# Normalising the input: gamma and beta as columns on transposed blocks, and a first product that goes through feature blocks

## The chip, the cores and the metric

The kernel runs on one core of one Trainium2 chip. The metric is the device time of one execution in microseconds, the median over several runs. A profile is one more execution, recorded instruction by instruction on the same core. The engines are TensorE (PE in the profile, its weight loads PEld), VectorE (DVE), ScalarE (ACT), GpSimd (POOL) and SyncE (SP), whose queue issues all loads here.

## What is computed

The reference is an encoder of two layers on x of 512 tokens by 1024 features. Cut to what matters:

```python
h = layer_norm(x, ln_in_g, ln_in_b)            # (x - mean) * rsqrt(var + 1e-5) * g + b, per token
for l in range(2):
    proj = h @ w_in[l]                         # 1024 x 4608, nine groups of columns
    # differential attention, a gated recurrence in both directions ("hg"), attention into mem
    h = layer_norm(ALPHA * h + mix @ w_out[l], ln1_g[l], ln1_b[l])
    # gated MLP with a depthwise convolution of width 3
    h = layer_norm(ALPHA * h + ffn, ln2_g[l], ln2_b[l])
```

The change concerns the first line and what uses it: `h` is needed twice, as the input of the first projections (features must lie on the partitions, as PE contracts over partitions) and as the residual (tokens on the partitions).

## The kernel before

**Numbers.** Every large product is made of three half-precision ones. A weight of 1 MB is loaded in f32 (`wst`, two buffers), its square is summed on ACT (L262), the sum goes through a tiny product on PE (`stat`, L165) to all partitions, DVE makes a power of two of it (L152 to L156), ACT writes the scaled high part `wh` (L265) and DVE the rest `wl` (L266). The activation has high and low parts `xh` and `xl` likewise, each [128, 8, 512]: feature block k, 512 tokens. A product is `wh·xh + wh·xl + wl·xh` (`mm3`).

**The first norm.** x lies in four tiles `z[0..3]` of 128 tokens by 1024 features. `layernorm(t, 0)` takes one tile: statistics (L222, L224), the reciprocal deviation `rs` in two instructions on POOL (L226, L227), then per half of 512 features two passes with gamma and beta, which lie in full tiles `mix` (a row loaded into all partitions, 512 KB each, L176). For tiles 0 and 1 both passes are on DVE (L235, L236). For tiles 2 and 3 (`LN_POOL`) DVE subtracts and scales (L231), and POOL multiplies by gamma and adds beta (L232, L233). Then PE transposes four blocks of 128 x 128 (L243), ACT writes `xh` with a scale (L247), and DVE `xl` (L248). Tile t is thus finished in `z[t]` for the residual and in `xh`, `xl` at once, and tile 0 can be used while tile 3 has not been touched.

**The first products.** `step_i` (columns 3072 and on of `w_in`, 256 wide) has tokens on the output's partitions: for tile t it runs the eight feature blocks of `wh·xh`, then of `wh·xl`, then of `wl·xh` (the `split` order of `gemm_t`), two tiles to a PSUM bank. `step_qf` takes the two weights after it; in each layer its first call runs the lower 256 tokens of its four outputs and then the upper 256. After it comes `step_fb` (full width, 512), then the keys and values of `mem`, whose blocks are transposed on PE as well (L339), and then the remaining projections. The attention parts are put between projections as a filler.

**What sets the order.** The program is written once in this order. Then a planner (`extract`, `deadlines`, `simulate`) takes all instructions, gives each a cost and a latest time worked back from PE's work, and fills each engine's queue in order of these times among what is ready; for loads it reckons with `DMA_RATE`. The program is built a second time with that order, and with the buffer slots that go with it, fixed for all five queues. So each engine works through its list in order, and a change of the code or of a cost moves instructions everywhere. `START` says what is emitted first: tile 0 of x, gamma and beta, the first weight, tiles 1 and 2, the second weight, tile 3. The order of emission decides between equal times, and who gets a buffer first.

The few lines that matter most, of the norm before:

```python
V.scalar_tensor_tensor(zt[:, c], zt[:, c], mv[:, 0:1], lng[:, c], ALU.subtract, ALU.mult)
V.scalar_tensor_tensor(zt[:, c], zt[:, c], rs, lnb[:, c], ALU.mult, ALU.add)
...
A.activation(xhs, pv, AF.Identity, scale=lnsc[:, idx : idx + 1])
```

## Time and profile before

| | |
|---|---|
| median of 3 runs | 1519.77 us (1518.19 to 1520.24) |
| profiled execution | 1518.81 us |
| its span on the core | 1517.0 us, 24771 instructions |
| mean granted clock of PE | 0.993 |
| loaded from memory | 138.23 MB |

The span is the time from the first to the last instruction of the record; the 1.8 us between it and the execution's time lie around it. A row of a group names the line, the engine, the operation, the tile written, the tiles read, the shapes and the count, then the busy time in us and the mean of one in ns, then the idle time ahead of it and what ended that. A row of the timeline begins with its start and its duration in us. A wait in brackets is the idle time of the engine before the row, and the releaser.

### The profile page before, as it was taken

What the parts mean: (1) busy time and instruction counts of PE and PEld (TensorE: products, weight loads), DVE (VectorE), ACT (ScalarE), POOL (GpSimd) and SP (SyncE); (2) the same over time, 40 slices, a digit from 0 to 9 for tenths busy, and PEclk for the clock granted to TensorE, in tenths of its full rate; (3) what the DMA queues carried; (4) which work ended last, traced back from release to release, by engine and by line L of the source; (5) the groups of instructions that cost most, each with busy time, mean ns of one, the idle gap of its engine ahead of it and who ended that gap; (6) DMA issues with size and microseconds to landing.
All of it is one profiled execution on the core that took longest, in us unless ns stands there. A gap on an engine that the chain in (4) does not pass through costs nothing. (4 is left out here: it accounts for less than half of the span.)

```text
span 1517.0 us, 24771 instructions
## 1 busy us (share of the span) xinstructions
PE 1458.1 (96%) x10072; PEld 823.6 (54%) x10072; DVE 1148.1 (76%) x2133; ACT 860.2 (57%) x1090; POOL 237.2 (16%) x258
## 2 busy tenths in 40 slices
PE   4999999998999999999999999999999999999997
PEld 3776565564574444444478475655555544444443
DVE  7688967868797766776695969678789767666777
ACT  4776555656366555554556556657653656455550
POOL 4131312030011001010110331021201101001011
PEclk9999999999999999999999999999999999999999
DMA  6332121222233333233234212021232333243321
GB/s 223 123 119 84 62 80 56 74 97 71 70 112 111 99 96 111 84 111 101 94 111 140 82 60 85 29 84 56 84 108 72 102 109 108 87 111 104 92 84 56
DMA packets 158141, 141.93 MB, mean 94 GB/s; under 512 B 3286, under 2 KB 139082, under 8 KB 158026
## 3 DMA queue, kind: packets, MB, share of 16 engines
q1 hardware_dynamic: 158026, 140.34, 29.6%
q8 instruction: 79, 1.29, 0.3%
q14 instruction: 36, 0.29, 0.1%
HBM read 138.23 MB, written 2.10 MB: 92 GB/s over the span
## 5 line engine op out<-in xcount | busy, mean ns | idle before, releaser
L137 PEld LDWEIGHTS <-wh 128*128 128x128 f16 x2688 | 256.9, 98 | 233.2 <-issue 3.8
L266 DVE SCALAR_TENSOR_TENSOR wl<-wst,ws,wh 128x2048 f16<-128x2048 f32 x122 | 315.9, 2590 | 72.1 <-ACT wh L265 71.8
L137 PE MATMUL mm<-xh,wl 128*128 128x512 f16 (+1 forms) x832 | 301.7, 363 | 1.3 <-DVE wl L266 1.3
L137 PE MATMUL mm<-xh,wh 128*128 128x512 f16 (+1 forms) x832 | 301.7, 363 | 0.0
L137 PE MATMUL mm<-xl,wh 128*128 128x512 f16 (+1 forms) x832 | 301.6, 363 | 0.0
L262 ACT ACTIVATE wh<-wst 128x2048 bf16<-128x2048 f32 x122 | 232.3, 1904 | 114.5 <-PE stat L165 50.7
L265 ACT ACTIVATE wh<-wst,ws 128x2048 f16<-128x2048 f32 x122 | 243.5, 1996 | 37.2 <-DVE wi L156 20.3
L137 PE MATMUL mm<-wh,t 128*128 128x512 f16 (+1 forms) x768 | 223.1, 370 | 1.7 <-DVE z L529 1.6
L137 PEld LDWEIGHTS <-wl 128*128 128x128 f16 x1344 | 131.6, 98 | 122.2 <-DVE wl L266 1.6
L137 PEld LDWEIGHTS <-t 128*128 128x128 f16 x1152 | 110.4, 98 | 122.1 <-issue 1.2
L529 DVE SCALAR_TENSOR_TENSOR z<-mm,inv,z 128x512 f32<-128x512 f32 x176 | 129.7, 745 | 46.3 <-PE mm L137 32.8
L137 PE MATMUL sc<-xh,wh 128*128 128x512 f16 (+1 forms) x448 | 156.2, 349 | 1.4 <-ACT xh L247 0.8
L137 PE MATMUL sc<-xh,wl 128*128 128x512 f16 (+1 forms) x448 | 156.2, 349 | 0.0
L137 PE MATMUL sc<-xl,wh 128*128 128x512 f16 (+1 forms) x448 | 156.2, 349 | 0.0
L1098 POOL TENSOR_TENSOR t<-f 128x512 f32<-128x512 f32 x44 | 58.1, 1321 | 547.1 <-DVE f L1096 438.5
L137 PE MATMUL mm<-wl,t 128*128 128x512 f16 (+1 forms) x384 | 142.1, 370 | 0.0
L152 DVE TENSOR_SCALAR we<-stat 128x1 int32<-128x1 int32 x122 | 18.4, 151 | 128.0 <-PE stat L165 127.8
L137 PE MATMUL mm<-wh,mgh 128*128 128x512 f16 x192 | 73.4, 382 | 7.8 <-DVE z L529 7.6
L1094 ACT ACTIVATE f<-sc,cvb,cw 128x512 f32<-128x512 f32 x44 | 34.1, 775 | 75.8 <-PE stat L165 72.3
L137 PE MATMUL mm<-wl,mgh 128*128 128x512 f16 x192 | 73.3, 382 | 0.0
L137 PE MATMUL mm<-wh,mgl 128*128 128x512 f16 x192 | 73.1, 382 | 0.0
L986 ACT ACTIVATE f<-sc,dam,iqk 128x512 f32<-128x512 f32 x64 | 49.3, 775 | 37.8 <-DVE dam L984 36.6
(224 smaller groups left out, 2190.5 us busy)
## 6 DMA issues: line engine op xcount, KB each, us to landing
wst<-in_w_up_dram SPq DMA_DIRECT2D x88, 512.0 KB, 4.3
wst<-in_w_in_dram SPq DMA_DIRECT2D x36, 1024.0 KB, 5.2
wst<-in_w_down_dram SPq DMA_DIRECT2D x22, 1024.0 KB, 5.1
wst<-in_w_out_dram SPq DMA_DIRECT2D x12, 1024.0 KB, 5.1
wst<-in_w_mem_kv_dram SPq DMA_DIRECT2D x8, 1024.0 KB, 4.9
z<-in_x_dram SPq DMA_DIRECT2D x4, 512.0 KB
mix<-in_ln_g_dram SPq DMA_DIRECT2D x4, 512.0 KB
mix<-in_ln_b_dram SPq DMA_DIRECT2D x4, 512.0 KB, 3.8
```

The lines of the kernel that those rows point to most:

```text
L137: T.matmul(o, lhsT, rhs, start=start, stop=stop)
L152: V.tensor_scalar(e, tot.bitcast(I32), 0x7F000000, 1, ALU.bitwise_and, ALU.logical_shift_right)
L262: A.activation(h.rearrange("p a b -> p (a b)").bitcast(BF16), flat, AF.Square, accum_out=ss)
L265: A.activation(h.rearrange("p a b -> p (a b)"), flat, AF.Identity, scale=s)
L266: V.scalar_tensor_tensor(l.rearrange("p a b -> p (a b)"), flat, s, h.rearrange("p a b -> p (a b)"), ALU.mult, ALU.subtract)
L529: V.scalar_tensor_tensor(zs, p_, ivs[half % len(ivs)], zs, ALU.mult, ALU.add)
L986: A.activation(pe[:, c, :], sc_[c], AF.Exp, bias=mx[:, c : c + 1], scale=iqk, accum_out=z1 if c else z0)
L1094: A.activation(c, p_, AF.Identity, scale=cw[:, 1, v : v + 1], bias=cvb[:, l, i + 22 * v : i + 22 * v + 1])
L1098: G.tensor_tensor(gt[:, n, :], c2[:, 0, :], c2[:, 1, :], ALU.mult)
```

## The change

- The first norm is a function of its own, `first_norm`. Each tile is only normalised, by one pass on DVE over 1024 features. When all four are done, each feature block k is transposed for all four tiles into one PSUM bank; features are then on the partitions, and ACT applies gamma and beta as columns (scale and bias) and writes f32 `w`; DVE writes `xh` from it and then `xl`.
- The columns `gbc` come from two loads of 4 KB and a transpose (`ln_columns`), and the scale of the first norm is now worked out from them, with a small product on PE.
- The residual gets its gamma and beta apart (`first_affine`): the full tiles are loaded later, and eight passes on DVE over 1024 features (multiply, then add, per tile) run in place on `z`. `proj_scale(0)`, which needs a square of the full gamma, moves with it, to after `step_qf`.
- `step_i` of the first layer has four outputs open, one per tile, in four PSUM banks, and goes through the feature blocks outermost: per block `wh·xh` and `wh·xl` for the four tiles, and after all blocks `wl·xh`.
- `step_qf` runs at full width in the first layer.
- `START`: constants and columns, the four tiles of x, then the two weights. The planner gets a `DMA_RATE` of 370e3 instead of 205e3, and the first nine loads are put ahead of all others.
- `LN_POOL` is gone. The sequence of units (`SEQ`, `LANE`, `LAST`) is now a table with the same content as before. Some small buffers are fewer.

```diff
-START = "0lw12v3"
-LN_POOL = [(0, 2), (0, 3)]
+START = "c0123wv"
...
+    def ln_columns():
+        rows = tmp([P, 160], "crow", bufs=1)
+        for i, v in enumerate(lngb[0]):
+            nc.sync.dma_start(rows[i * KT : (i + 1) * KT, 0:P], v.rearrange("(k p) -> k p", p=P))
+        pt = ptr()
+        T.transpose(pt[:, 0 : 2 * KT], rows[0 : 2 * KT, 0:P], ident[0 : 2 * KT, 0 : 2 * KT])
+        V.tensor_copy(gbc.rearrange("p i k -> p (i k)"), pt[:, 0 : 2 * KT])
...
+        T.matmul(tot, ones, ss.bitcast(BF16)[:, 1:4:2], start=True, stop=True)
+        both = small(2, "gbto", bufs=1)
+        V.tensor_copy(both, tot)
+        ln_scale(both, 0)
+        V.tensor_scalar(gbc, gbc, lnsc[:, 0:1], None, ALU.mult)
+
+    def first_norm():
+        for t in range(TT):
+            mu, rs = norm(t, 0)
+            V.tensor_scalar(z[t], z[t], mu, rs, ALU.subtract, ALU.mult)
+        for k in range(KT):
+            pt = ptr()
+            for t in range(TT):
+                T.transpose(pt[:, t * P : (t + 1) * P], z[t][:, k * P : (k + 1) * P], ident)
+            w = tmp([P, S], "w2", bufs=4)
+            A.activation(w, pt, AF.Identity, scale=gbc[:, 0, k : k + 1], bias=gbc[:, 1, k : k + 1])
+            V.tensor_scalar(xh[:, k, :], w, 1.0, None, ALU.mult)
+            V.tensor_tensor(xl[:, k, :], w, xh[:, k, :], ALU.subtract)
+
+    def first_affine():
+        load_ln(0)
+        for t in range(TT):
+            for j, op in enumerate((ALU.mult, ALU.add)):
+                V.tensor_tensor(z[t], z[t], lngbt[j], op)
...
             def step_qf(ws):
-                if pr == 0:
+                if pr == 0 and l:
...
             def step_i(ws):
-                hs["v"] = yield from tok_out(ws[0], "tokv", l == 0 and pr == 0)
+                if l or pr:
+                    hs["v"] = yield from tok_out(ws[0], "tokv")
+                    return
+                hv = hs["v"] = tmp([P, 4, 256], "tokv", bufs=2)
+                w, iv = ws[0], inv_of(ws[0], xin)
+                ps = [pmm("mm" if t % 2 == 0 else "sc")[:, 0:256] for t in range(TT)]
+                for u, xs in ((w.h, xact), (w.l, xact[:1])):
+                    for k in range(KT):
+                        for n, d in enumerate(xs):
+                            for t in range(TT):
+                                mm(ps[t], d[:, k, t * P : (t + 1) * P], u[:, k, :], u is w.h and k + n == 0, u is w.l and k == KT - 1)
...
-DMA_RATE = 205e3
+DMA_RATE = 370e3
...
+    for k, o in enumerate([o for o in ops if o.dmab][:FIRST]):
+        D[o.i] = k - 1000.0
```

How this moves instructions is seen in each engine's list. SP's list, at the start of the program; `z` are the tiles of x, `wst` weights, `mix` the full gamma and beta, `crow` small rows. Before:

```order
L257 DMA wst_119<-in_w_in_dram 128x8x256
L212 DMA z_77<-in_x_dram 128x1024
L176 DMA mix_100<-in_ln_in_g_dram 128x1024
L176 DMA mix_104<-in_ln_in_b_dram 128x1024
L140 DMA cst<-in_consts_dram 128x132
L212 DMA z_78<-in_x_dram 128x1024
L212 DMA z_79<-in_x_dram 128x1024
L257 DMA wst_136<-in_w_in_dram 128x8x256
L212 DMA z_80<-in_x_dram 128x1024
```

and now:

```order
L143 DMA cst<-in_consts_dram 128x132
L240 DMA crow_99<-in_ln_in_g_dram 8x128
L240 DMA crow_99<-in_ln_in_b_dram 8x128
L218 DMA z_77<-in_x_dram 128x1024
L218 DMA z_78<-in_x_dram 128x1024
L218 DMA z_79<-in_x_dram 128x1024
L218 DMA z_80<-in_x_dram 128x1024
L302 DMA wst_129<-in_w_in_dram 128x8x256
L302 DMA wst_144<-in_w_in_dram 128x8x256
L178 DMA mix_621<-in_ln_in_g_dram 128x1024
```

The four tiles of x moved ahead of both weights, and the full gamma behind them. On DVE, at the second weight's low part (`wl_148` before, `wl_156` now; its product is the first of `step_qf`). Before, `z_80` is the last tile of x and `xl<-tr_225` belongs to the third:

```order
L248 SCALAR_TENSOR_TENSOR xl<-tr_215,lnsc,xh 128x4x128
L463 COPY rpf_1549<-qsc 128x1
L231 TENSOR_SCALAR z_80<-z_80,bnmv_235,lnrs_237 128x512 x2
L266 SCALAR_TENSOR_TENSOR wl_148<-wst_136,ws_144,wh_138 128x2048
L248 SCALAR_TENSOR_TENSOR xl<-tr_225,lnsc,xh 128x4x128
L401 TENSOR_TENSOR w_57_316<-w_56_314 128x256
```

and now, where the rows on `z` are affine passes with gamma, and the last two feature blocks stand some fifteen rows ahead of these:

```order
L443 TENSOR_REDUCE lsum<-w_66_323 128x4
L458 CAST masks<-crow_617 128x160
L272 TENSOR_TENSOR z_77<-z_77,mix_621 128x1024
L155 TENSOR_SCALAR we_344<-stat 128x1
L272 TENSOR_TENSOR z_78<-z_78,mix_621 128x1024
L311 SCALAR_TENSOR_TENSOR wl_156<-wst_144,ws_152,wh_146 128x2048
```

All of `xl` now stands ahead of the second weight's low part, and two affine passes stand between. On PE, at the first transposes. Before, tile 0's two banks are followed by products at once:

```order
L165 MATMUL stat<-wss_122,ones 128x1
L243 MATMUL tr_162<-cst,z_77 128x128 x4
L243 MATMUL tr_171<-cst,z_77 128x128 x4
L137 LDWEIGHTS xh
L137 MATMUL mm_361<-wh_121,xh 128x256
```

and now, where `tr_195` and `tr_204` are feature blocks 0 and 1, each with a piece of all four tiles:

```order
L262 MATMUL tr_195<-cst,z_79 128x128
L262 MATMUL tr_204<-cst,z_79 128x128
L168 LDWEIGHTS ones
L168 MATMUL stat<-wss_132,ones 128x1
L262 MATMUL tr_195<-cst,z_80 128x128
L262 MATMUL tr_204<-cst,z_80 128x128
L262 MATMUL tr_213<-cst,z_77 128x128
```

The sum of the first weight's square (`stat<-wss_132`) moved from the head of PE's list to behind the third tile's transposes, and no product stands ahead of the fourth tile's. The sum of the third weight's square, `stat<-wss_341`, stands among the products of `wl`, after the first five.

More of the change, by code (lines that the diff above doesn't have):

```diff
@@ L169, in trunk @@
     lnsq = [None, None]
-    hold = [None]
     def load_ln(idx):
@@ L247, in layernorm @@
                 A.activation(xhs, pv, AF.Identity, scale=lnsc[:, idx : idx + 1])
-                hold[0] = V.scalar_tensor_tensor(xls, pv, lnsc[:, idx : idx + 1], xhs, ALU.mult, ALU.subtract).ins
+                V.scalar_tensor_tensor(xls, pv, lnsc[:, idx : idx + 1], xhs, ALU.mult, ALU.subtract)
     def prep(src, shape):
@@ L378, in setup_gates @@
             A.activation(e1, e1, AF.Exp)
-            zz = small(4, "lbz")
+            zz = small(4, "lbz", bufs=2)
             V.tensor_tensor(zz, e0, e1, ALU.add)
@@ L458, in scale_rope @@
     def scale_rope(l):
-        f = small(1, "rpf")
+        f = small(1, "rpf", bufs=1)
         if l:
@@ L719, in step_qf @@
                 for i in range(4):
-                    if pr == 0:
+                    if pr == 0 and l:
                         p_ = ps[i]
@@ L1040, in build_layer @@
         if l == 0:
-            add([], lambda ws: [layernorm(t, 0) for t in range(TT)] and None)
-            add([], lambda ws: late(setup_gates))
-            add([], lambda ws: late(proj_scale, 0))
+            add([], lambda ws: first_norm())
+            add([], lambda ws: setup_gates())
         else:
             add_mkv(l)
-        hg_units(0)
-        if l == 0:
-            add([], lambda ws: setup_rope())
-        add([], lambda ws: scale_rope(l))
-        hg_units(1)
-        mx_units(0)
-        mx_units(1)
-        da_units(0)
-        add_wout("hg", 0)
-        da_units(1)
-        add_wout("hg", 1)
-        add_wout("da", 0)
+        for name, *arg in SEQ[l]:
+            if name == "rope":
+                if l == 0:
+                    add([], lambda ws: setup_rope())
+                add([], lambda ws: scale_rope(l))
+            elif name == "out":
+                add_wout(*arg)
+            else:
+                {"hg": hg_units, "mx": mx_units, "da": da_units}[name](*arg)
         ol = {}
@@ L1494 @@
 PEN = 20.0
+FIRST = 9
 def deadlines(ops, tiles):
```

88 lines of the change are left out of this document (51 added, 37 removed).

## The prediction

> **What bounds the kernel now.** I read the page's busy times first, then the same in stretches, then the waits of TensorE (PE).
>
> ```profile
> PE 1458.1 (96%) x10072; PEld 823.6 (54%) x10072; DVE 1148.1 (76%) x2133; ACT 860.2 (57%) x1090; POOL 237.2 (16%) x258
> 0.00:20.00 20.00, 3.29 (x15) 2.48 (x16) 11.32 (x25) 8.63 (x10) 2.93 (x10) 1.00 0.92 327
> 20.00:40.00 20.00, 15.38 (x117) 11.26 (x116) 17.66 (x42) 11.29 (x20) 15.24 (x12) 1.00 0.35 111
> 40.00:60.00 20.00, 20.00 (x186) 17.74 (x185) 11.15 (x45) 14.23 (x18) 0.00 (x0) 1.00 0.35 112
> 60.00:80.00 20.00, 18.35 (x157) 10.84 (x156) 17.43 (x35) 14.38 (x17) 5.26 (x5) 0.93 0.33 107
> 80.00:120.00 40.00, 39.80 (x609) 28.10 (x607) 35.27 (x76) 28.47 (x36) 15.05 (x18) 0.99 0.42 139
> ```
>
> The columns of the stretches are PE, PE's weight loads, VectorE (DVE), ScalarE (ACT), GpSimd (POOL), granted clock, DMA share, GB/s. PE is busy 1458.1 of 1517.0 us, so 58.9 us of idle PE are all that can be won without less work. Of these 21.3 lie in the first 40 us (16.71 + 4.62); from 40 us on PE is full. The change is about these 40 us, so the question is when PE becomes full. The timeline of PE shows its waits there, and where the step after the first two products begins.
>
> ```profile
> 14.78 1.97 PE L243 MATMUL tr<-cst,z 128*128 128x128 f32 x8 [6.65 <-DVE z L236]
> 18.85 1.89 PE L137 MATMUL mm<-wh,xh 128*128 128x256 f16 x8 [2.10 <-ACT xh L247]
> 20.53 2.02 PE L137 MATMUL mm<-wh,xl 128*128 128x256 f16 x8
> 22.34 0.60 PE L137 MATMUL mm<-wl,xh 128*128 128x256 f16 x3
> 34.52 0.28 PE L137 MATMUL mm<-xh,wl 128*128 128x256 f16 x1 [1.33 <-DVE wl L266]
> 37.04 0.66 PE L243 MATMUL tr<-cst,z 128*128 128x128 f32 x4 [0.94 <-POOL z L233]
> 61.13 0.27 PE L137 MATMUL sc<-xl,wh 128*128 128x256 f16 x1
> 61.24 0.27 PE L137 MATMUL sc<-xh,wl 128*128 128x256 f16 x1
> 61.35 0.38 PE L137 MATMUL mm<-xh,wh 128*128 128x512 f16 x1
> 61.57 0.38 PE L137 MATMUL mm<-xl,wh 128*128 128x512 f16 x1
> ```
>
> The last wait ends at 37.04. At 61.35 the first 512-wide product starts: that is `step_fb`, so `step_i` and `step_qf` are done. 61.35 is my mark: whatever is before it, the same step must begin in the changed kernel, and the gain is the difference. Spacing gives a product's price on a full PE: 0.11 us at width 256 (61.13 to 61.24), 0.216 at 512 (61.35 to 61.57 and on).
>
> **The change, part by part.** First the start of the data.
>
> ```profile
> 0.72 0.43 SPq L257 DMA_DIRECT2D wst<-in_w_in_dram  x1
> 10.40 0.25 SPq L363 DMA_DIRECT2D crow<-in_da_norm_g_dram  x1
> 5.91 1.91 ACT L262 ACTIVATE wh<-wst 128x2048 bf16<-128x2048 f32 x1 [3.91 <-DMA wst<-in_w_in_dram]
> 8.24 1.28 DVE L222 BATCH_NORM_STATS2 bnst<-z 128x6 f32<-128x512 f32 x2
> GB/s 7 311 390 307 398 416 362 373 384 322 119 350 100 0 0 4 8 26 359 140 41 0 0 0 136 378 42 303 221 0 0 0 110 377 50 274 250 0 0 8
> ```
>
> (GB/s in slices of 2 us.) Before, the first 1 MB weight is issued at 0.72 and usable 5.19 us later; x's first tile is worked on at 8.24. Now the constants (0.43) and two small loads (0.25 each) go ahead, and x's first tile (0.5 MB) is issued at about 1.9. At about 360 GB/s half a MB less is 1.45 us less: usable at 1.9 + 5.2 − 1.45 = 5.6, the next ones 1.45 apart (10.0 for the fourth). The weights follow at about 12.8 and 15.7 (1 MB is 2.9 us more each). The first one's square ends near 14.9, and the blocks need ACT only at 17, so I cost that at nothing; a weight 2 us later would show in full. The two loads of gamma and beta as full tiles move behind the weights and are hidden.
>
> Now the durations, from the groups by shape, and the spread of three of them.
>
> ```profile
> L222 DVE BATCH_NORM_STATS2 bnst<-z 128x6 f32<-128x512 f32 x40 | 27.0, 685 | 0.2
> L224 DVE BATCH_NORM_AGGREGATE bnmv<-bnst 128x2 f32<-128x12 f32 x20 | 4.1, 205 | 0.1
> L505 DVE TENSOR_SCALAR mgh<-mix,gs 128x1024 f16<-128x1024 f32 x12 | 9.5, 795 | 0.2
> L696 DVE TENSOR_SCALAR f<-sg 128x512 f32<-128x512 f32 x16 | 6.8, 424 | 0.3
> L950 DVE TENSOR_TENSOR sg<-sg,mm 128x512 f32<-128x512 f32 x16 | 10.9, 682 | 5.9 <-POOL sg L948 5.9
> L760 DVE TENSOR_TENSOR t<-f,qg 128x1024 f32<-128x1024 f32 x8 | 15.6, 1956 | 0.0
> L154 DVE TENSOR_SCALAR ws<-we 128x1 int32<-128x1 int32 x122 | 18.3, 150 | 2.9
> L266 DVE SCALAR_TENSOR_TENSOR wl<-wst,ws,wh 128x2048 f16<-128x2048 f32 x122 | 315.9, 2590 | 72.1 <-ACT wh L265 71.8
> L1094 ACT ACTIVATE f<-sc,cvb,cw 128x512 f32<-128x512 f32 x44 | 34.1, 775 | 75.8 <-PE stat L165 72.3 <-PE sc L137 3.5
> L265 ACT ACTIVATE wh<-wst,ws 128x2048 f16<-128x2048 f32 x122 | 243.5, 1996 | 37.2 <-DVE wi L156 20.3 <-DVE ws L154 13.3 <-DVE ge L152 3.3
> L328 ACT ACTIVATE t<-t 128x512 bf16<-128x512 f32 x4 | 2.5, 622 | 0.0
> L226 POOL TENSOR_SCALAR lnrs<-bnmv x20: 221/777/785, 9.9 to 1510.7; 128x1 f32<-128x1 f32 x20
> L227 POOL TENSOR_TENSOR lnrs<-lnrs,mhalf x20: 567/578/2524, 10.7 to 1511.5; 128x1 f32<-128x1 f32 x20
> L231 DVE TENSOR_SCALAR z<-z,bnmv,lnrs x4: 536/542/1492, 22.0 to 30.6; 128x512 f32<-128x512 f32 x4
> L236 DVE SCALAR_TENSOR_TENSOR z<-z,lnrs,mix 128x512 f32<-128x512 f32 x36 | 26.1, 744 | 2.7 <-POOL lnrs L227 2.7
> ```
>
> Step 1, to the fourth normalised tile, on DVE: 8 statistics at 0.64 (two took 1.28) = 5.1; 4 aggregates, 0.8; 4 subtract-and-scale passes 1024 wide, which the trace lacks: between 0.80 (L505, one scalar) and 1.08 (two L231), I take 0.85 = 3.4, near the row of the same width; seven one-column operations of the gamma scale at 0.15 = 1.05; 0.9 for waits on POOL's `rs` (0.22 + 0.57 when free). 5.6 + 11.25 = 16.9.
>
> The pair on POOL is where a rule speaks against the change. L231 took up to 1.49 beside POOL's work and 0.54 free. The Trainium skill, "SBUF — State Buffer", "Who interferes with whom", says that such a DVE pass and GpSimd lock each other out of a shared port for a whole instruction. By it the last `rs` waits for a pass, 0.85 more, and the sum below would be 3.5 instead of 4.4. I keep the row of the free pair, since PE's order needs the last `rs` only once.
>
> Step 2: all four tiles must be there before any block is, unlike before, where tile 0 alone gave products at 18.85. Transposes 0.5, two blocks on ACT at 0.775 (L1094, PSUM with scale and bias columns), the weight's `wh` 2.0: 20.9. Then DVE makes this weight's `wl` ahead of the other six blocks: 2.5 (2.59 mean, 2.35 at best): 23.4.
>
> Step 3: six blocks of 0.42 (L696) + 0.68 (L950), overlapping by 0.06, 1.04 each: 29.7. PE's part (8 products and 4 transposes a block, 1.3) runs beside it.
>
> Step 4: ACT from 20.9: six blocks 4.65, the second weight's square 2.0, four squares of `mem` 2.5, the third weight's square 2.0: 32.1. PE's order puts the sum of that square after five of the 32 `wl` products, so 27 × 0.109 = 2.95 remain, and four transposes of `mem`, 0.45: PE begins `step_qf` at 35.5.
>
> Step 5: DVE from 29.7: eleven one-column operations at 0.15 and three of 256 columns or fewer at 0.4, near L696's row, 2.8 in all; two of the new affine passes, 2.4 (one 1024 wide taken as twice L950 less one overhead, 1.22; L760 shows 1.96 with POOL beside it, and POOL has nothing then), then the second weight's `wl` 2.5: 37.4. PE needs it after four products, at 36.4, and waits 1 us.
>
> Step 6: 92 products of 0.216 remain: 19.9. `step_fb` starts at 57.3 instead of 61.35, 4.0 sooner, and four transposes (0.44) that stood behind it are done. **Gain 4.4 us.**
>
> Cheap ends of the rows (0.80, 2.35, blocks overlapping more) give 5.6; dear ones (1.08, 0.78 for every L226, 2.59, no overlap) 1.9. Neither end falls below zero, because x arrives 2.6 us sooner than before.
>
> The other edits. Work that goes off the path: six more affine passes (7.3 us of DVE) lie in 38 to 56 us, where DVE has 8.85 us free (40 to 60). POOL loses its passes over z, and with them the wait at 37.04:
>
> ```profile
> L232 POOL TENSOR_TENSOR z<-z,mix 128x512 f32<-128x512 f32 x4 | 8.2, 2058 | 2.2 <-DVE z L231 2.2
> L233 POOL TENSOR_TENSOR z<-z,mix 128x512 f32<-128x512 f32 x4 | 5.2, 1312 | 0.0
> ```
>
>  Joining the half-wide products of `step_qf` leaves 0.2. `DMA_RATE` and `FIRST` move weight loads and reorder nearly every engine later on; two buffers hold the weights either way, so I cost that at 0, between −2 and +2: 37.6 us of idle PE (58.9 − 21.3) lie after 40 us, and the largest group there is eight waits for DVE's residual adds:
>
> ```profile
> PE mm L137 <- DVE z L529: 9.1, 8, 2.7
> ```
>
> **The rivals.** First, the gain is given back at the memory products. DVE has 9.2 us more to do (8 affine passes 9.8, 8 for `xh` 3.4, 4 normalising 3.4, the scale 1.0; gone are 8 passes like L236, 5.9, and four L231, 2.5 of them) and was 87% busy from 60 to 80, where PE already waited here:
>
> ```profile
> 76.76 0.71 PE L339 MATMUL tr<-cst,t 128*128 128x128 f32 x4 [1.33 <-issue]
> ```
>
> In its new order DVE has from 37.4 to the last piece of `mem`: five `wl` 12.7, six affine passes 7.3, one L760 1.96, 21 passes of about 0.6 (L696, L950) 12.4, and 54 small operations, 5.9 where they overlap (0.11): 40.3, so 77.7. PE, running free, wants that piece 18.5 after `step_fb` starts (its 48 products 10.4, then 8.1), at 75.8. With the small ones at 0.15 it is ready at 79.9. So PE waits 1.9 to 4.1 instead of 1.3: at the worst 2.8 lost, 1518.2, and with the dear ends of the start 1520.7. Against it: before, DVE's idle time there is mostly waiting for ACT and PE, which now come sooner. Chance 0.23.
>
> Second, slower: the affine passes run at L760's 1.96, 5.9 us more in all. This decides if POOL reads SBUF beside them; POOL's order has nothing between the four `rs` and the gate chain, so that it needs passes slipping past 60 us. Then DVE is the bound up to the gate chain: 15.1 us more work against 8.85 free leaves 6.3 late, 2.8 more at `mem`, less 4.4: 4.7 slower, 1524.5. Chance 0.10.
>
> Third, a clock that stays low. At 18.85 and 20.53 sixteen products took 3.49 us, 0.218 each, twice the 0.109 they take from 22.34 on, though the granted clock reads 1.00. In the new order products come in bursts behind blocks. If they stay at 0.218 until the blocks end, 64 products are 14.0 and 16 transposes 4.0: 39.0 instead of 30.1, less the slack of 2 us before the sum in step 4, 7 late: 1522. The Trainium skill, "TensorE: Matmul & The Clock Gate", "What's actually happening", has PE at half clock until a window of about 3.4 us was busy; the trace's 3.49 agrees. Against the rival: at half speed a block costs PE 2.7 us and DVE 1.04, so PE is busy without a gap and warms up by 24.5, inside the slack. Chance 0.05.
>
> Fourth, later waits shrink with the new order: 2 to 4 us more, 1511 to 1513. Chance 0.10.
>
> **How the numbers follow.** The profiled execution took 1518.81, 0.96 below the median of 1519.77. Span 1517.0 − 4.4 = 1512.6, with 1.8 around it 1514.4; against the median 1519.77 − 4.4 = 1515.4. The forecast has 0.52. Its own bounds are 1513.5 to 1518 (gain 1.9 to 5.6, and the reorder). The range takes in the fourth case's 1511, the first one's 1520.7 and the near half of the slow cases: 1510.5 to 1521.5. About 0.2% (3 us) is what a measurement of this kernel tells from no change. Faster by that means below 1516.7: most of the forecast, all of the fourth: 0.59. Slower means above 1522.8: 0.12. Same: 0.29.
>
> **What would show it.** Right: x's first statistics at 5 to 6; the fourth pass done by 17 to 18; last `xl` near 30; `step_fb` at 56 to 59; DVE busier than 18 of 20 us from 20 to 60. Wrong: first block after 20; PE waiting over 3 us for `wl` near 36 or for `mem` near 75; products 0.218 apart after 27; idle PE after 100 us that differs by more than 3 us.

## The result and the profile after

| | before | after |
|---|---|---|
| median of the runs | 1518.99 us (1518.19 to 1520.24) | 1531.96 us (1528.92 to 1533.23) |
| profiled execution, span | 1518.81, 1517.0 | 1531.11, 1529.3 |
| PE busy, mean granted clock | 1458.1, 0.993 | 1463.1, 0.992 |
| PE idle in the first 100 us | 23.2 | 16.6 |
| PE idle after that | 35.7 | 49.6 |

The changed kernel is slower: ratio 1.0082, 95% interval 1.0064 to 1.0100. (A fourth run brings the median of the kernel before from 1519.77 to 1518.99. One execution of `rate_back` and one of `wl_cost`, both below, ran at a granted clock of 0.943 and 0.698; these two count in the medians and not in the ratios.) The forecast was 4.4 us less; it is 13 us more. The last two rows say where to look. The start won 6.6 us, more than forecast, and everything behind it lost: 13.9 us of waits and 5.0 us of PE's busy time (−6.6 + 13.9 + 5.0 = 12.3, the difference of the spans).

First the start. The busy line and the stretches of the changed kernel, same columns as before (PE, PEld, DVE, ACT, POOL, clock, DMA share, GB/s):

```profile
PE 1463.1 (96%) x9978; PEld 813.2 (53%) x9978; DVE 1141.4 (75%) x2146; ACT 861.7 (56%) x1092; POOL 231.9 (15%) x250
```

```profile
0.00:20.00 20.00, 6.05 (x24) 3.93 (x25) 13.53 (x37) 7.58 (x8) 3.88 (x14) 1.00 0.86 319
20.00:40.00 20.00, 20.00 (x149) 14.96 (x148) 19.90 (x53) 17.87 (x32) 0.00 (x0) 1.00 0.38 126
40.00:60.00 20.00, 20.00 (x97) 9.12 (x96) 18.35 (x51) 14.39 (x16) 0.00 (x0) 1.00 0.49 158
60.00:80.00 20.00, 17.36 (x221) 13.03 (x220) 19.11 (x29) 16.68 (x20) 10.38 (x6) 1.00 0.33 107
80.00:120.00 40.00, 40.00 (x598) 25.05 (x596) 35.68 (x84) 29.18 (x40) 8.17 (x18) 1.00 0.34 113
```

PE is now full from 20 to 60 us, where before it was full only from 40 on; from 60 to 80 it is idle for 2.6 us, a little more than the 1.7 of before. The steps one by one, in the timeline of the changed kernel:

```profile
5.58 1.29 DVE L227 BATCH_NORM_STATS2 bnst<-z 128x6 f32<-128x512 f32 x2 [1.27 <-DMA z<-in_x_dram]
12.54 2.60 DVE L258 TENSOR_SCALAR z<-z,bnmv,lnrs 128x1024 f32<-128x1024 f32 x3
12.97 0.46 POOL L231 TENSOR_SCALAR lnrs<-bnmv 128x1 f32<-128x1 f32 x1
13.52 0.77 POOL L232 TENSOR_TENSOR lnrs<-lnrs,mhalf 128x1 f32<-128x1 f32 x1
25.93 1.29 DVE L266 TENSOR_TENSOR xl<-w,xh 128x512 f16<-128x512 f32 x2
31.52 2.35 DVE L311 SCALAR_TENSOR_TENSOR wl<-wst,ws,wh 128x2048 f16<-128x2048 f32 x1
33.28 0.38 PE L140 MATMUL mm<-xh,wh 128*128 128x512 f16 x1
```

The four normalised tiles are there at 15.1 (12.54 + 2.60), the last `xl` at 27.2, the second weight's `wl` at 33.9, and `step_qf` begins at 33.28. With 96 products of 0.216 it ends at 54.0, and `step_fb` begins at 54.05, where before it began at 61.35.

Now the rest. Three groups of PE's waits after the first 100 us grew (us in all, times, longest):

```profile
PE mm L140 <- DVE z L569: 14.6, 11, 2.7
PE tr L168 <- ACT t L536: 5.5, 4, 1.5
PE stat L168 <- ACT wh L307: 4.0, 7, 1.1
```

Before, the first of them was 9.1 (the eight waits for the residual adds in the prediction), and of the other two there was nothing of note in that stretch. That is 15 us more, about the 13.9 of all waits together. The last two come from ACT. These are the waits of ACT ahead of a weight's square, by what ended them, of the kernel before and of the changed one (us, times):

```profile
  DMA wst<-in_w_up_dram: 11.0, 4
  DMA wst<-in_w_in_dram: 6.5, 3
  DMA wst<-in_w_mem_kv_dram: 2.1, 1
```

```profile
  DMA wst<-in_w_up_dram: 36.4, 18
  DMA wst<-in_w_down_dram: 18.8, 8
  DMA wst<-in_w_in_dram: 16.5, 7
  DMA wst<-in_w_out_dram: 2.4, 2
  DMA wst<-in_w_mem_kv_dram: 0.5, 2
```

19.6 us of waits for weights have become 74.5 (10.1 of them stand at the very start, where x goes first). The loads are no slower: where the trace shows a landing, it came 3.6, 4.8 and 6.2 us after the issue (the least, the median and the most of 40 loads, half of them of 512 KB), against 3.9, 5.0 and 11.7 before (23 loads). The squares stand where the loads have not landed yet. What that does is seen in the second MLP, in SP's queue of loads of the kernel before, then of the changed one:

```profile
1306.26 10.41 SPq L257 DMA_DIRECT2D wst<-in_w_down_dram  x2
1368.60 10.41 SPq L257 DMA_DIRECT2D wst<-in_w_down_dram  x2
1430.94 31.15 SPq L257 DMA_DIRECT2D wst<-in_w_down_dram  x4
```

```profile
1310.85 10.41 SPq L302 DMA_DIRECT2D wst<-in_w_down_dram  x2
1376.52 9.76 SPq L302 DMA_DIRECT2D wst<-in_w_down_dram  x2
1441.52 30.50 SPq L302 DMA_DIRECT2D wst<-in_w_down_dram  x4
```

One round of six weights took 62.34 us before, both times, and takes 65.7 and 65.0 now. PE was busy for the whole of those 62.34; now it is idle for 2.2 us of each round, 1.48 of them in one wait. These are all PE waits over 1 us after 1200 in the changed kernel:

```profile
1233.44 0.38 PE L140 MATMUL mm<-wh,t 128*128 128x512 f16 x1 [1.27 <-DVE z L569]
1357.25 0.16 PE L168 MATMUL tr<-gss,ones 128*128 128x1 bf16 x1 [1.48 <-ACT t L536]
1422.25 0.16 PE L168 MATMUL tr<-gss,ones 128*128 128x1 bf16 x1 [1.48 <-ACT t L536]
1487.03 0.16 PE L168 MATMUL tr<-gss,ones 128*128 128x1 bf16 x1 [1.05 <-ACT t L536]
```

### The profile page after: what moved, and what is told of

Same layout as the page of the kernel before. It is cut to its first block, busy times and chain, and to the rows that moved or that the text cites. A ratio compares the mean times of both kernels' runs of the same rounds, so it can differ in the third digit from the quotient of the medians.

```text
span 1529.3 us, 24599 instructions
## 1 busy us (share of the span) xinstructions
PE 1463.1 (96%) x9978; PEld 813.2 (53%) x9978; DVE 1141.4 (75%) x2146; ACT 861.7 (56%) x1092; POOL 231.9 (15%) x250
## 5 line engine op out<-in xcount | busy, mean ns | idle before, releaser
L311 DVE SCALAR_TENSOR_TENSOR wl<-wst,ws,wh 128x2048 f16<-128x2048 f32 x122 | 307.0, 2518 | 100.1 <-ACT wh L310 99.8
L140 PEld LDWEIGHTS <-wh 128*128 128x128 f16 x2624 | 250.8, 98 | 241.8 <-issue 8.1
L140 PE MATMUL mm<-xl,wh 128*128 128x512 f16 (+1 forms) x832 | 306.3, 368 | 0.0
L140 PE MATMUL mm<-xh,wh 128*128 128x512 f16 (+1 forms) x832 | 306.2, 368 | 0.1
L140 PE MATMUL mm<-xh,wl 128*128 128x512 f16 (+1 forms) x832 | 306.1, 368 | 0.0
L310 ACT ACTIVATE wh<-wst,ws 128x2048 f16<-128x2048 f32 x122 | 243.4, 1996 | 28.8 <-DVE ws L157 14.0
L569 DVE SCALAR_TENSOR_TENSOR z<-mm,inv,z 128x512 f32<-128x512 f32 x176 | 129.9, 745 | 47.3 <-PE mm L140 34.3
L1151 POOL TENSOR_TENSOR t<-f 128x512 f32<-128x512 f32 x44 | 66.0, 1500 | 558.3 <-DVE f L1149 282.8
L140 PE MATMUL sc<-xh,wl 128*128 128x512 f16 (+1 forms) x416 | 147.4, 354 | 0.0
L140 PE MATMUL sc<-xl,wh 128*128 128x512 f16 (+1 forms) x416 | 147.4, 354 | 0.0
L140 PE MATMUL sc<-xh,wh 128*128 128x512 f16 (+1 forms) x416 | 147.4, 354 | 0.0
L140 PE MATMUL mm<-wh,mgh 128*128 128x512 f16 x192 | 73.8, 384 | 12.3 <-DVE z L569 12.3
L1150 ACT ACTIVATE f<-f 128x512 f32<-128x512 f32 x44 | 27.7, 630 | 83.2 <-DVE f L1149 74.6
L1042 ACT ACTIVATE f<-sc,dam,iqk 128x512 f32<-128x512 f32 x64 | 49.2, 775 | 29.6 <-DVE dam L1040 29.6
```

Of the source, the lines that this page charges most:

```text
L140: T.matmul(o, lhsT, rhs, start=start, stop=stop)
L310: A.activation(h.rearrange("p a b -> p (a b)"), flat, AF.Identity, scale=s)
L311: V.scalar_tensor_tensor(l.rearrange("p a b -> p (a b)"), flat, s, h.rearrange("p a b -> p (a b)"), ALU.mult, ALU.subtract)
L569: V.scalar_tensor_tensor(zs, p_, ivs[half % len(ivs)], zs, ALU.mult, ALU.add)
L1042: A.activation(pe[:, c, :], sc_[c], AF.Exp, bias=mx[:, c : c + 1], scale=iqk, accum_out=z1 if c else z0)
L1150: A.activation(c2[:, 0, :], c2[:, 0, :], AF.Silu)
```

## The experiments

The theory before these runs: with `DMA_RATE` at 370e3 the planner reckons 4.9 us for 1 MB (bytes over the rate plus 2.1), with 205e3 it reckons 7.2. The 2.3 us between them were a margin, and without it ACT's squares stand where their loads are not there yet. The rivals: `FIRST`, the new passes and steps themselves, and a new order that is worse by chance. "ACT's wait" is its idle time before squares that a load ended; PE's idle time is that after the first 100 us; both are from the profiled execution. Ratios are to the kernel before in the same set of runs.

| kernel | rate | time, us | ratio (95%) | ACT's wait | PE idle |
|---|---|---|---|---|---|
| before | 205e3 | 1518.99 | 1 | 19.6 | 35.7 |
| after | 370e3 | 1531.96 | 1.0082 (1.0064–1.0100) | 74.5 | 49.6 |
| rate_back | 205e3 | 1515.37 | 0.9965 (0.9951–0.9979) | 14.7 | 35.7 |
| before_rate | 370e3 | 1548.34 | 1.0177 (1.0154–1.0200) | 84.2 | 52.6 |
| first_off | 370e3 | 1533.14 | 1.0081 (1.0064–1.0098) | 74.6 | 50.0 |
| rate_back_first_off | 205e3 | 1514.04 | 0.9960 (0.9950–0.9970) | 22.6 | 36.6 |
| rate_sim_back | 205e3 in the run through time | 1514.63 | 0.9963 (0.9948–0.9978) | 15.0 | 35.4 |
| rate_due_back | 205e3 in the latest times | 1525.83 | 1.0035 (1.0022–1.0048) | 77.1 | 46.6 |
| rate_290 | 290e3 | 1514.47 | 0.9953 (0.9939–0.9967) | 44.1 | 35.6 |
| rate_150 | 150e3 | 1541.72 | 1.0141 (1.0123–1.0160) | 14.0 | 41.7 |
| rate_mlp_back | 205e3 for the MLP | 1517.14 | 0.9986 (0.9977–0.9996) | 34.3 | 37.9 |
| no_affine | 205e3 | 1515.66 | 0.9976 (0.9966–0.9986) | 14.4 | 36.5 |
| tile_order | 205e3 | 1518.39 | 0.9990 (0.9977–1.0003) | 14.2 | 34.5 |
| before_290 | 290e3 | 1531.66 | 1.0074 (1.0057–1.0091) | 52.7 | 40.6 |
| squares_later | 370e3 | 1599.64 | 1.0525 (1.0504–1.0545) | 12.3 | 90.0 |
| squares_earlier | 205e3 | 1692.13 | 1.1140 (1.1119–1.1160) | 113.4 | 159.0 |
| squares_later_205 | 205e3 | 1613.44 | 1.0618 (1.0598–1.0638) | 0.2 | 97.3 |
| before_290_later | 290e3 | 1601.93 | 1.0539 (1.0518–1.0561) | 35.1 | 91.1 |
| fifteen_later | 370e3 | 1537.21 | 1.0094 (1.0077–1.0112) | 30.3 | 53.1 |
| wl_cost | 370e3 | 1520.43 | 0.9996 (0.9986–1.0007) | 54.0 | 40.1 |

### Which edit

```diff
-DMA_RATE = 370e3
+DMA_RATE = 205e3
```

> The changed kernel with DMA_RATE back at 205e3, all else as changed. Theory (the rate): with 370e3 the planner reckons 1 MB to be there in 2.8 + 2.1 us and places the loads later, so that ACT waits for weights (71 us in all before its squares, against 20 in the kernel before) and PE for what ACT and DVE then do late; with the old rate these waits fall to about 20 and the start's gain (6.6 us less idle PE in the first 100 us) is left: 1512 to 1514. Rival one (FIRST): no change, about 1530. Rival two (the new passes and steps themselves disturb the later part): about 1530, with ACT's waits for weights near 20 all the same. Rival three (any new order moves the later waits by chance): anything from 1508 to 1530.

Measured 1515.37: the loss of 13 us is a gain of 5, and PE's idle time after 100 us is that of before to the tenth, 35.7. The waits for weights in it:

```profile
  DMA wst<-in_w_up_dram: 12.4, 5
  DMA wst<-in_w_mem_kv_dram: 2.1, 1
  DMA wst<-in_w_in_dram: 0.2, 1
```

In the kernel before, the other way round (205e3 to 370e3, nothing else):

> The kernel before with DMA_RATE at 370e3 and nothing else. Theory (the rate): ACT's waits for weights rise from 20 us to 60 or more, and the time to 1530 to 1538 (the same loss of 13 + 6.6 us without the start's gain). Rivals one and two: 1517 to 1521, since neither FIRST nor the new passes are in it. Rival three: some time from 1512 to 1530 with no tie to ACT's waits for weights.

1548.34, 10 us above the expected range: the number alone costs this kernel 27 us. `FIRST`, with the new rate and with the old one:

```diff
-FIRST = 9
+FIRST = 0
```

> The changed kernel with FIRST = 0, so that the first nine loads are no longer put ahead of all others; DMA_RATE stays at 370e3. Theory (the rate): the later waits stay, 1529 to 1536, a little worse at the start where the weights may again go ahead of x. Rival one (FIRST, which puts the loads of the first weights before everything and so shifts what follows): 1512 to 1516. Rival three: anything from 1508 to 1535.

> The changed kernel with both planner edits undone: DMA_RATE 205e3 and FIRST = 0. What is left is the new norm, the new first product, and full width in the second step. Theory (the rate): the later waits are gone, but the order of the first loads is the planner's: 1512 to 1518. Rival two (the steps themselves): about 1530 again. Rival one: 1512 to 1516, as without FIRST alone.

1533.14 and 1514.04: `FIRST` makes no difference that these runs can tell. The rate does it, and neither `FIRST` nor the new steps. A chance order is not excluded by any single run, but it is a poor rival: the five plans of the changed kernel in this table whose run through time reckons with 205e3 and whose lists were left as planned lie 0.10 to 0.40% below the kernel before, and the two that reckon with 370e3 throughout, other costs as before, 0.81 and 0.82% above.

### Which use of the number, and which size

The planner uses the rate twice: in `simulate`, its run through time that makes the lists, and in `deadlines`, for the latest times by which it ranks them. Each was set to 205e3 apart:

```diff
 # rate_sim_back
-            dma_free = d0 + o.dmab / DMA_RATE
+            dma_free = d0 + o.dmab / 205e3
 # rate_due_back
-                x -= o.dmab / DMA_RATE + 2
+                x -= o.dmab / 205e3 + 2
```

> The changed kernel; the planner's run through time (simulate) takes a load's duration from 205e3 again, the latest times (deadlines) stay with 370e3. Theory (margin): the old rate makes the planner believe that 1 MB lands 7.2 us after its issue, where the trace shows 4.8 in the median; the 2.4 us that are left over are the margin that keeps ACT's squares behind other ready work in its list, so that a late load holds nothing up. Then the figure in the run through time alone brings it back: 1513 to 1517, ACT's waits for weights 15 to 25 us. Rival (due times: with the higher rate the loads get later due times and are issued later): about 1530, with waits of 60 us or more.

> The other half: the latest times from 205e3, the run through time at 370e3. Theory (margin): nothing is won, 1528 to 1536, ACT's waits for weights 60 to 85 us. Rival (due times): 1513 to 1517 and waits of 15 to 25 us.

The run through time brings back all of it. The latest times bring back a part, 0.47% or 7 us, against the expectation, and without less waiting on ACT (77.1): a sum of waits is not a price. Of the 7.6 us between the two profiled spans, 4.7 are PE's busy time (1458.4 and not 1463.1, at a granted clock of 0.997 and not 0.992) and 2.9 its idle time; why the clock is higher there stays open. Then the size:

> The changed kernel with DMA_RATE = 290e3 in both places: the planner reckons 5.7 us for 1 MB, 0.9 above the 4.8 that the trace shows, where 205e3 gives 7.2 (2.4 above) and 370e3 gives 4.9 (0.1 above). Theory (margin): between the two, 1516 to 1527, ACT's waits between 20 and 70 us. Rival (a chance order): no tie between the rate and the time.

> The changed kernel with DMA_RATE = 150e3: 9.1 us reckoned for 1 MB, 4.3 more than it takes. Theory (margin): the waits for weights fall further, below 15 us, and the time is 1511 to 1518, unless the squares now come so late in ACT's list that PE waits for their sums: then up to 1525. Rival (a rate near the real one is best for the planner): worse than with 205e3, as far from the truth on the other side, 1520 to 1535.

290e3 was as good as 205e3, and at 150e3 the time rose to 1541.72, though ACT waited least for loads of all the rates (14.0). There PE waits for what follows from late squares. Half of the loss stands in the start: 29.6 us of idle PE in the first 100 us, 18.1 in rate_back. Two waits of the 150e3 kernel that rate_back does not have:

```profile
61.41 0.61 PE L140 MATMUL mm<-xh,wh 128*128 128x512 f16 x1 [3.10 <-ACT wh L310]
97.40 0.39 PE L140 MATMUL mm<-t,wh 128*128 128x256 f16 x2 [1.17 <-ACT wh L310]
```

So for the changed kernel there is a valley with two walls: 4.9 us and 9.1 us, as reckoned for 1 MB, lose; 5.7 and 7.2 do not. Where the wall at 4.9 stands was tried with the old rate for the MLP's weights alone:

```diff
+            if any(x in str(ins[0].tensor.name) for x in ("w_up", "w_down")):
+                n *= 370 / 205
```

> The changed kernel with 370e3, but the loads of w_up and w_down (the MLP) are reckoned at the old 205e3, all others at 370e3. Theory (margin, lost in the MLP, where each weight's square, the pieces of the convolution and the high parts share ACT's list): most of the loss returns, 1512 to 1518, with ACT's waits for weights of w_up and w_down below 15 us instead of 55, and the early start of the 370e3 plan kept (PE 83 us busy in the first 100). Rival (the loss lies in the projections and attention, 20 to 360 and 780 to 1100 us): 1524 to 1531.

1517.14: 0.96% of the 1.17% between the two rates comes back, in the MLP.

### How it comes about

In the lists of the two rates, the same stretch of ACT's list in the second MLP. `wh_13384` with `wss_13385` is a weight's square, L1147 a piece of the convolution, L310 the high part of the weight before. At 370e3:

```
L1150 ACTIVATE f_2303_13295<-f_2303_13295 128x512
L307 ACTIVATE wh_13384,wss_13385<-wst_13382 128x2048
L310 ACTIVATE wh_13306<-wst_13304,ws_13312 128x2048
L1147 ACTIVATE f_2303_13295<-sc_13242,cvb,cw_13293 128x512
```

and at 205e3:

```
L1150 ACTIVATE f_2303_13295<-f_2303_13295 128x512
L1147 ACTIVATE f_2303_13295<-sc_13242,cvb,cw_13293 128x512
L310 ACTIVATE wh_13306<-wst_13304,ws_13312 128x2048
L307 ACTIVATE wh_13384,wss_13385<-wst_13382 128x2048
```

The square has gone two places ahead. The same place in the timeline of the changed kernel, and then the same place with the old rate:

```profile
1325.11 0.17 PE L168 MATMUL stat<-wss,ones 128*128 128x1 bf16 x1
1325.98 1.91 ACT L307 ACTIVATE wh<-wst 128x2048 bf16<-128x2048 f32 x1 [2.77 <-DMA wst<-in_w_down_dram]
1327.89 1.99 ACT L310 ACTIVATE wh<-wst,ws 128x2048 f16<-128x2048 f32 x1
1329.78 0.76 ACT L1147 ACTIVATE f<-sc,cvb,cw 128x512 f32<-128x512 f32 x1
1329.91 2.35 DVE L311 SCALAR_TENSOR_TENSOR wl<-wst,ws,wh 128x2048 f16<-128x2048 f32 x1 [3.90 <-ACT wh L310]
```

```profile
1303.64 10.41 SPq L302 DMA_DIRECT2D wst<-in_w_down_dram  x2
1317.90 0.17 PE L168 MATMUL stat<-wss,ones 128*128 128x1 bf16 x1
1318.11 0.78 ACT L1147 ACTIVATE f<-sc,cvb,cw 128x512 f32<-128x512 f32 x1 [2.11 <-PE stat L168]
1318.78 1.99 ACT L310 ACTIVATE wh<-wst,ws 128x2048 f16<-128x2048 f32 x1
1320.68 1.90 ACT L307 ACTIVATE wh<-wst 128x2048 bf16<-128x2048 f32 x1
```

Take PE's `stat` as the zero of both. The load of this weight (the second of its row in SP's queue, 10.04 after the first: 10.41 less 0.37 for its own issue) is issued 4.2 us ahead of it in both kernels, so the load is no later in one than in the other. With the old rate the convolution's piece follows `stat` 0.2 later, the high part 0.9, the square 2.8. With the new one the square comes at 0.9, when its load lands, 0.7 after the piece could have run; the high part comes at 2.8, the piece at 4.7, and `wl` waits 3.90 for that high part. The planner gives an engine the most urgent of what is ready by its reckoning: with the load at 4.9 us the square got the place ahead of the piece, with 7.2 it did not. A load of 4.9 us issued 4.2 ahead of `stat` would land 0.7 behind it, though, when the piece could have run at 0.2. So the plan must have had the load earlier against `stat`, or ACT free later, than the trace has them; the plan's own times are not on record. Further down the same round PE waits 1.48 for the square of `t`, which the pieces make (1357.25 above).

That a square which waits holds up what is behind it can be read here; whether ACT's list alone makes the loss cannot. So the squares were moved in ACT's finished list, with the other four lists left as they were:

```diff
+    for i in sorted(squares):
+        k = act.index(i) + MOVE        # +1: squares_later, -1: squares_earlier
...
+        act[act.index(i)], act[k] = act[k], i
```

> The changed kernel at 370e3; after planning, each weight's square on ACT changes places with the instruction behind it in ACT's list where nothing forbids it (109 of 122). The lists of DVE, PE, POOL and SP stay as they are. Theory (a square that waits for its load holds up ready work behind it): ACT's waits for weights fall from 74.5 to 30 to 45 us, and the time from 1532 by 5 to 12 us, to 1520 to 1527. Rival (all lists fit the early squares, and moving one of them only makes the sums later): 1532 to 1545.

> The changed kernel at 205e3, with each square one place earlier in ACT's list (114 of 122), all other lists as they are. Theory: ACT's waits for weights rise from 15 to 50 us or more, and the time from 1515 to 1520 to 1530. Rival: no change within 3 us, or faster, since the sums come sooner.

> The control: the changed kernel at 205e3 with each square one place later in ACT's list (108 of 122). The loads are there in time already (15 us of waits), so by the theory nothing is to be won: 1515 to 1535, the slower the more the sums become late for PE, as at 150e3 (1541.7). If this is faster too, a later square is good for another reason than the loads.

> The kernel before at 290e3 (1531.7, ACT's waits for weights 53 us) with each square one place later in ACT's list. Theory: waits of 25 us or less, 1520 to 1528. Rival (its loss of 12 us at 290e3 has another cause, as its 6 us of lower clock and later residual adds): 1530 to 1545.

All four lost 68 to 177 us against the same kernel unmoved. Earlier, the waits for loads were as expected or worse (113 us). Later, they fell (to 12.3, 0.2 and 35.1), and PE waited for the sums in their place, since its own list still has these where the planner put them. The largest group of PE's waits of squares_later (us in all, times, longest):

```profile
PE stat L168 <- ACT wh L307: 56.7, 34, 3.6
```

My expectation for the later ones was wrong, and the control lost as much at the old rate, so a move of nearly all squares tells nothing of the loads. The finer try moved just fifteen squares of the MLP, those that had waited over 2 us and had two other instructions behind them:

> The changed kernel at 370e3; fifteen squares of w_up and w_down, those that waited over 2 us for their load in its trace (42.8 us in all) and have two other instructions behind them, go two places later in ACT's list, behind a piece of the convolution and the high part of the weight before; nothing else moves. Theory (these held up what stood behind them): the waits for loads fall from 74.5 to 25 to 35 us, and the time from 1532 by 6 to 13 us, to 1519 to 1526. Rival (the sums of these squares are needed where they stood): PE's waits for stat rise by as much or more, 1532 to 1545.

```diff
+HELD = (37, 42, 47, 49, 54, 59, 61, 98, 103, 108, 110, 114, 116, 120, 122)
+    for n in HELD:
+        i = squares[n - 1]
+        k = act.index(i)
+        act[k : k + 3] = act[k + 1 : k + 3] + [i]
```

ACT's waits fell as expected, to 30.3, and the time did not: 1537.21. PE now stood at four places like the first row here, and three of the four waits for `t` stayed, as in the second:

```profile
1352.72 0.16 PE L168 MATMUL stat<-wss,ones 128*128 128x1 bf16 x1 [2.25 <-ACT wh L307]
1426.96 0.16 PE L168 MATMUL tr<-gss,ones 128*128 128x1 bf16 x1 [1.36 <-ACT t L536]
```

So the theory falls in its narrow form. It is not the wait on ACT alone that costs the time: PE's list was written for the early squares as well, and mending one list moved the wait to the next. What the margin of the old rate covered is then a question about the plan. The load's own figure is one part of it at most. For weights in one piece 4.9 us is about right (4.8 to 5.2 in the median, by weight). The MLP's `w_up` comes in two pieces of 512 KB, and the eighteen squares that waited for it began 5.2 to 6.6 us after the first issue, 5.4 in the median, where the plan reckons 4.9. These 0.5 us are less than the 2.0 that each of these squares waited on average. Another candidate is the pass that frees a weight's buffer for the next load, `wl`, which the plan reckons at 2.26 us. Four rows of the changed kernel, two places at which it meets POOL's pass:

```profile
1317.45 1.27 POOL L1151 TENSOR_TENSOR t<-f 128x512 f32<-128x512 f32 x1 [29.93 <-DVE f L1149]
1317.63 3.24 DVE L311 SCALAR_TENSOR_TENSOR wl<-wst,ws,wh 128x2048 f16<-128x2048 f32 x1 [0.35 <-ACT wh L310]
734.14 2.34 DVE L311 SCALAR_TENSOR_TENSOR wl<-wst,ws,wh 128x2048 f16<-128x2048 f32 x1
734.37 3.24 POOL L1151 TENSOR_TENSOR t<-f 128x512 f32<-128x512 f32 x1 [11.99 <-DVE f L1149]
```

Whoever begins second takes longer: `wl` 3.24 and not 2.34, or POOL 3.24 and not 1.27. This is not new in the changed kernel (23 of its 122 `wl` take over 2.8 us, and 31 in rate_back); so by this candidate the new rate took away the slack in the plan, and the overlap was there before. The last run gave the planner 0.9 us more for such passes and left the rate at 370e3:

```diff
-        return (0.125 if kind == "InstTensorScalarPtr" and two else 0.068) + n / 960.0, 0.09
+        return (0.125 if kind == "InstTensorScalarPtr" and two else 0.068) + n / 960.0 + (0.9 if two and n == 2048 else 0), 0.09
```

> The changed kernel at 370e3, where the planner reckons 0.9 us more for each pass of 2048 columns with two full operands on DVE (above all wl: 3.16 instead of 2.26; the trace has 2.32 to 3.35, 2.52 in the mean). The buffer of a weight then comes free later in the plan, and the next load is issued later in it. Theory (the margin covers other costs that the plan takes too low): ACT's waits for weights fall from 74.5 to below 45 us, and the time from 1532 to 1514 to 1522. Rival (the loads themselves need the margin): 1527 or more.

1520.43: 0.86% of the 1.17% is back without touching the rate, and the round in the second MLP is at its old length (62.44, then 62.40):

```profile
1307.59 12.48 SPq L302 DMA_DIRECT2D wst<-in_w_down_dram  x2
1370.03 12.48 SPq L302 DMA_DIRECT2D wst<-in_w_down_dram  x2
1432.43 33.10 SPq L302 DMA_DIRECT2D wst<-in_w_down_dram  x4
```

ACT's waits fell less than expected (54.0, not below 45). So the margin need not be in the load's figure. That it is `wl`'s overlap with POOL that must be covered, and not any 0.9 us in that chain, was not tried apart, and neither was a figure of its own for `w_up`. What the plan reckons too low is thus open; that its figure for the load decides the loss is shown.

### The new steps

```diff
 # no_affine
-        for t in range(TT):
-            for j, op in enumerate((ALU.mult, ALU.add)):
-                V.tensor_tensor(z[t], z[t], lngbt[j], op)
```

> The changed kernel with the old rate (205e3), without the eight passes that apply gamma and beta to the residual of the first norm; the loads of the full gamma and beta stay. Leaves out: gamma and beta in the first residual. Forecast (the passes lie in DVE's free time): within 2 us of the kernel with the old rate and the passes (1515.4), the wait of 2.2 us for the last piece of mem near 74 us shorter by up to 2.2. Rival (DVE becomes the bound up to the gate chain): 3 to 6 us faster, 1509 to 1512.

This kernel leaves gamma and beta out of the first residual. It took 1515.66 beside 1515.37: the eight passes cost nothing that these runs can tell.

```diff
 # tile_order
-                for u, xs in ((w.h, xact), (w.l, xact[:1])):
+                hs["v"] = yield from tok_out(ws[0], "tokv", l == 0 and pr == 0)
```

> The changed kernel with the old rate (205e3) and the first product in the order of before: tile by tile, per tile eight blocks of the high part, eight of the low part, then the low part of the weight. The new norm stays, so that no tile is complete before the last feature block. Theory (the order over feature blocks is what lets PE work while the blocks come): the products start after the last block, near 31 instead of 22.8, and 64 products of 0.109 (7.0 us) are no longer hidden behind the blocks: 1519 to 1523, PE busy 75 to 77 us of the first 100. Rival (DVE and ACT set the pace of the start, and the second weight is only ready at 36 anyway): within 2 us of 1515.4.

The first product was at 21.97, not at 31: tile 0's products follow the blocks as well. The median is 3 us over that of rate_back, the two intervals overlap at their ends, and the profiled execution shows no loss (span 1512.4, PE idle 19.0 in the first 100 us against 18.1). What the order over feature blocks is worth stays open.

Last, the kernel before with 290e3:

> The kernel before with DMA_RATE = 290e3 and nothing else. The changed kernel gained 17 us from 370e3 to 290e3 and nothing more from 290e3 to 205e3 (1514.5 and 1515.4). Theory (a threshold: the plan works as long as it reckons a little more than the load takes): 1516 to 1523, as with 205e3. Rival (the kernel before stands on its rate by a chance order): 1525 to 1540.

1531.66, the rival's case. The kernel before loses 0.74% (11 us) at a rate that costs the changed one nothing. In the profiled executions 8.4 of 13.1 us are PE's busy time (1466.5 against 1458.1, at a clock of 0.989 and not 0.993). Why its plan has less room was not found. One difference can be read from the traces: the squares that waited for `w_up` began 5.8 us after the first issue here (the median of 19), and 5.4 in the changed kernel at the same rate (of 10), where the plan reckons 5.7. That this makes the difference was not tried.

## Why the prediction was wrong

- **Step 1** (four tiles at 16.9): 15.1. A pass took 0.81, and where 0.9 was set down for waits on `rs`, each of the last three passes began 0.07 after DVE was free. The Trainium skill, "SBUF — State Buffer", "Who interferes with whom", by which the last `rs` would have waited for a whole pass (0.85), is borne out in kind and not in price: beside the passes POOL's two instructions took 0.46 + 0.77, not 0.22 + 0.57, and each ended less than 0.1 after a pass did (passes at 13.35 and 14.25, POOL at 13.43 and 14.29). The last `rs` came 0.44 later by this, and the passes lost 0.2 in all.
- **Steps 2 to 5**: right in their order and 2 to 3.5 us early, 1.8 of it from step 1. The rest goes, as I read it, to squares that stand earlier at the new rate: the first one begins at 12.1, and at 17.5 with the old rate. With the old rate `step_qf` begins at 36.72, 1.2 later than forecast, and `step_fb` at 58.47, with eight transposes of `mem` (0.9) among the 96 products; the forecast had 57.3.
- **Step 6, gain 4.4**: the right order of size for the start, and in part by luck. In the changed kernel `step_fb` begins 7.3 us sooner, not 4.0, and PE's idle time in the first 100 us is 6.6 less. With the old rate it begins 2.9 sooner; rate_back gains 0.35%, 5.3 us, and its idle PE is 5.1 us less in the first 100 us and the same behind them. But the steps were read from the lists of the new rate, and rate_back runs others. This version, and rate_back_first_off, rate_sim_back and rate_290 with it, beat both kernels.
- **The step that failed** is the sentence on the other edits: "`DMA_RATE` and `FIRST` move weight loads and reorder nearly every engine later on; two buffers hold the weights either way, so I cost that at 0, between −2 and +2". It measured 17.8 us (1.0082 − 0.9965, of 1519). The reason given was about when loads can start, which indeed did not change at the place looked at (4.2 ahead of `stat` in both). But the rate also says when the planner thinks that they end, and all lists are filled by that. The range for it was set beside the 37.6 us of idle PE after 40 us: such a pool bounds a gain, and no loss.
- **First rival** (given back at `mem`): in the changed kernel PE waits 0.46 for a piece of `mem`, at 67.70, and not at all for the last, which is there at 73.7 (at 74.23 it waits 1.91 for POOL). With the old rate it waits 2.23 for the last piece but one. That lies between the 1.9 and 4.1 worked out, but by luck: DVE has the last piece at 74.2 and not at 77.7 to 79.9, and PE comes to its wait at 71.4 and not at 75.8. The 8.1 behind the 48 products in that sum stands in no row. **Second** (the passes at 1.96): they took 1.22. **Third** (a low clock): products were 0.21 apart until 21.4 and 0.11 from 21.9 on, inside the slack. **Fourth** (later waits shrink): they grew. None of the four had the case that came: a reckoned load time nearer to the truth that makes the plan worse.
- Of the signs of being wrong, idle PE after 100 us that differs by over 3 us was the one that came: 13.9. Of the signs of being right, the first statistics (5.58) and a busy DVE (19.9 and 18.35 of 20) came, and the others came earlier than set out.

## What to carry to other kernels

An edit of a cost that a scheduler reckons with is a change to every list it writes, and deserves a term of its own with a wide range, above all towards a loss. A figure that is nearer to the truth can make a plan worse, as here, where the old one left a margin; look for what is reckoned too low beside it, and change such a figure in a run of its own. When a wait is read off one in-order engine, the test is to move that instruction alone: here the wait went and the time stayed.

## What the runs showed of the hardware

- `wl` on DVE and `t` on POOL do not run side by side: at the two places above the second one took 0.9 and 2 us longer. Over the whole changed kernel, the 81 `wl` with no POOL instruction beside them took 2.32 to 2.35, the 12 that began ahead of POOL's the same, and 23 of the 29 that began during one over 2.8, up to 3.35. The Trainium skill, "SBUF — State Buffer", "Who interferes with whom", says that a DVE instruction with two SBUF inputs contends with POOL's reads and that the first one issued blocks the other; the rows agree.
- PE's busy time is not a constant of the work. The same 9978 instructions took 1460.6 us in rate_back at a mean granted clock of 0.992 and 1509.4 in squares_earlier at 0.962 (3.3% more at a clock 3.0% lower), the kernel with the most waits: 159.0 us of idle PE after the first 100 us, against 35.7. In the four kernels with 90 us or more the waits came with a clock of 0.962 to 0.982, so there they were paid once as idle time and again as clock. Between 35 and 53 us no such tie can be told: the runs of before_rate alone, one kernel, go from 0.988 to 0.995. The Trainium skill, "TensorE: Matmul & The Clock Gate", "What's actually happening", calls the throttled state the default, which activity releases; the two runs agree with that.
